# Sums on VectorE issued later in mixer A's values, and the first token tile scaled by its gain behind the transposes

## The chip, the cores and the metric

The kernel runs on one core of one Trainium2 chip. A core has five engines that run their own instruction streams side by side: TensorE (PE, matmuls and transposes), VectorE (DVE), ScalarE (ACT), GpSimd (POOL) and SyncE (SP, which here only issues DMAs). The metric is device time in microseconds (us), as the median of several executions. Besides, one execution was profiled.

## The reference

A two-layer encoder on x of 512 tokens by 1024 channels, float32. Each layer is a token mixer and a squared-ReLU MLP, each behind an RMS norm. Layer 0 has mixer A, attention in three groups of eight heads of 128 columns with different dilations; layer 1 has mixer B, latent attention. Cut to what matters here:

```python
h = rms_norm(x, norm_mix[0])              # x * rsqrt(mean(x*x) + 1e-6) * gain
qkv = (h @ w_qkv).reshape(B, S, 3, N_GROUPS, A_HEADS, A_HEAD_DIM)
for g, (window, dil) in enumerate(DIL_CONFIGS):
    q = rope(rms_norm(qkv[:, :, 0, g], q_gain[g]), S)
    k = rope(rms_norm(qkv[:, :, 1, g], k_gain[g]), S)
    v = qkv[:, :, 2, g]
    o, lse = dilated_group(q, k, v, window, dil)
...
x = x + (o @ w_o);  x = x + sq_relu_mlp(rms_norm(x, norm_ffn[0]), w1, w2)
```

The change touches the norm of x and the product that gives v.

## The kernel before, in words

**Tiling.** The 512 tokens lie in four tiles of 128 rows (r = 0 to 3). A tile is normed by `norm(r)`: ScalarE squares and sums a row (L138), VectorE adds epsilon (L130, `rs_v`), GpSimd raises to the power -0.5 (L133, `nrs`), and one VectorE instruction multiplies x by this scale and by the gain table, a row of 1024 gains copied to all partitions by a DMA (L376, `xn`). `turn(r)` transposes the tile on TensorE in two halves of four 128x128 blocks (L125, into a bank `tp`), so that the channels lie on the partitions.

**Splitting.** Every product is made of three matmuls on rounded operands: hi·hi, hi·lo and lo·hi. ScalarE makes the rounded hi by a copy, and VectorE subtracts it from the value to give lo. For the tokens this is L388 and L389 (`hT`); for weights it is `split_w` (L421 and L422, `whi` and `wlo`, in four buffers each), or L158 and L159 for head 6. For the first two tiles ScalarE also keeps the unrounded turned tile (L392, `h32`).

**The values.** `v_phase` makes v of heads 0 to 5 with a product of 2 by 2 blocks in seven products instead of eight (Strassen's scheme in Winograd's form). The blocks of the weights of a group g are b11, b21, b12 and b22, each 512 rows by 384 columns, loaded in two pieces (L343, 384 KB each). Some products use sums of blocks: bT = b11+b12, then bT+b22, then bT+b21, and b3 = b12+b22. `add_block` (L346) makes such a sum in two VectorE instructions. On the token side sums `Ssp` are made once. The products run in the order 2, 1, 5, 3, 6, 7, 4; each has two halves u of the weights and two blocks t of the tokens. They accumulate in three pairs of banks: `acc` (product 2), `sc` (products 1, 6, 7 and 4) and `tp` (products 5 and 3). `put` (L447) drains a bank into `vo`, by a copy on ScalarE (L453) or an addition or subtraction on VectorE (L455), and a DMA of GpSimd's queue stores the result. After product 6 the `sc` banks are subtracted from `vo`, and product 7 goes on adding to the same banks, so it has to wait for the drain; the same holds between products 7 and 4. `piece(g, ba)` holds products 5 to 4 of a group. Head 6 of all groups is made by a plain product (`block_groups`, L191) between products 1 and 5 of group 0; its weights (`raw`) come in four pairs of DMAs, and the last pair comes last.

**What sets the order.** A scheduler places the instructions of each engine from the program and a model of their times; `tc.issue_after(x)` adds the rule that what stands in it is issued after x. On its engine an instruction then runs strictly in the place given. SP issues its DMAs in order, and each waits until the one eight places before has landed. In the program, the sums of a group stand behind products 2 and 1 of that group, but the scheduler places an instruction as soon as its inputs are expected, so they could move ahead into the group before. After product 1 of group 1, `tables(0)` makes four products for attention A's rotary tables (L271 and L274).

## Time and profile before

| | |
|---|---|
| median of three runs | 1404.27 us (1403.55 to 1405.62) |
| the profiled execution's own time | 1403.76 us |
| its span in the trace | 1402.0 us |
| TensorE busy | 1371.6 us, 98% |
| VectorE busy | 940.0 us, 67% |
| values (`v_phase`) | from the start to about 120 us |
| attention A's first part | 124 to 540 us |

In rows of the waits the columns are: who waited (engine, operation, line), for whom, the sum in us, how often, and the longest. In rows of windows: the window, its length, then for each engine its busy time and instructions, the granted TensorE clock, the busy share of the DMA engines, and GB/s. In rows of a timeline: start, length, engine, line, operation, output and inputs, shapes, count, and in brackets how long the engine was idle before and what ended it.

### The profile page before, as it was taken

How to read it: one execution, taken by the hardware profiler on the slowest of the kernel's cores; microseconds unless marked ns; L12 is line 12 of the kernel's file. 1: busy time of each engine (PE TensorE's matmuls, PEld its weight loads, DVE VectorE, ACT ScalarE, POOL GpSimd, SP SyncE). 2: the span in 40 equal slices, each digit the busy share in tenths (PEclk: the TensorE clock that was granted, in tenths of full speed). 3: DMA queues.
4: the chain of work that ended last, by engine and by line, in shares of the span. 5: the costliest groups of instructions: out<-in, count | busy, mean ns of one | idle time of the engine just before them, and what ended most of it. 6: DMA issues, size and time to landing. Idle time of an engine off the chain costs nothing.

```text
span 1402.0 us, 18979 instructions
## 1 busy us (share of the span) xinstructions
PE 1371.6 (98%) x6852; PEld 1163.6 (83%) x6852; DVE 940.0 (67%) x1498; ACT 801.0 (57%) x1643; POOL 224.0 (16%) x240
## 2 busy tenths in 40 slices
PE   7999999999999999999999999999999999999998
PEld 6999887888889989888888878777769888888887
DVE  6886777787788744464655768788745465574747
ACT  6544778687786624453536455777534553644543
POOL 1110212121122001020200204433201020020101
PEclk9999999999999999999999999999999999999999
DMA  9535553655555539486583944211116668493835
GB/s 309 170 134 163 134 130 97 164 131 125 143 130 120 158 106 271 135 186 174 123 237 87 234 96 95 61 31 31 46 46 189 172 131 230 98 234 119 198 88 120
DMA packets 171774, 197.83 MB, mean 141 GB/s; under 512 B 59104, under 2 KB 109024, under 8 KB 171680
## 3 DMA queue, kind: packets, MB, share of 16 engines
q1 hardware_dynamic: 152496, 157.55, 37.7%
q0 software_dynamic: 19184, 39.07, 15.5%
q8 instruction: 54, 0.88, 0.3%
q14 instruction: 40, 0.33, 0.1%
HBM read 176.13 MB, written 7.86 MB: 131 GB/s over the span
## 4 chain that ended last, share of the span: by engine, by line
PE 80%; DVE 7%; DMA 4%; issue 4%; ACT 3%; POOL 1%; SPq 0%; ACTq 0%; DVEq 0%; POOLq 0%
PE acc L191 49%; PE sc L877 9%; PE tp L877 6%; PE sc L436 3%; PE tp L125 2%; DMA wqs<-in_ffn_w_dram 2%; PE acc L1170 1%; DVE wlo L820 1%; PE sc L1064 1%; DMA xT<-t 1%; PE acc L1146 1%; PE tp L436 1%; PE sc L602 1%; PE sco L716 1%; PE sco L712 1%
## 5 line engine op out<-in xcount | busy, mean ns | idle before, releaser
L191 PE MATMUL acc<-whi,hT 128*128 128x512 f32 (+2 forms) x1208 | 377.2, 388 | 1.9 <-ACT hT L761 1.0
L191 PE MATMUL acc<-hT_f,whi 128*128 128x512 f32 (+1 forms) x1152 | 317.5, 366 | 0.0
L159 DVE TENSOR_TENSOR wlo<-raw,whi 128x1024 fp32r<-128x1024 f32 (+3 forms) x146 | 172.8, 1188 | 169.3 <-ACT whi L158 168.8
L191 PEld LDWEIGHTS acc<-whi,hT 128*128 128x128 f32 x1208 | 224.4, 188 | 42.7 <-ACT hT L761 1.7
L158 ACT ACTIVATE whi<-raw 128x1024 fp32r<-128x1024 f32 (+3 forms) x146 | 149.7, 1029 | 159.6 <-PE acc L191 74.8
L191 PEld LDWEIGHTS acc<-hT_f,whi 128*128 128x128 f32 x1152 | 207.9, 189 | 34.9
L191 PE MATMUL acc<-wlo,hT 128*128 128x512 f32 (+2 forms) x604 | 232.9, 386 | 0.4 <-DVE wlo L159 0.4
L820 DVE TENSOR_TENSOR wlo<-wqs,whi 128x1024 fp32r<-128x1024 f32 x112 | 137.7, 1231 | 114.0 <-ACT whi L819 113.9
L819 ACT ACTIVATE whi<-wqs 128x1024 fp32r<-128x1024 f32 x112 | 118.3, 1060 | 162.0 <-PE acc L191 66.2
L191 PE MATMUL acc<-hT_f,wlo 128*128 128x512 f32 (+1 forms) x576 | 204.1, 366 | 0.0
L877 PE MATMUL sc<-whi,asp 128*128 128x512 f32 x512 | 165.1, 390 | 1.0 <-DVE resid L851 1.0
L805 POOL DMA_DIRECT2D wqs<-in_ffn_w_dram x64 | 77.7, 1347 | 539.7 <-DVE wlo L820 358.1
L191 PEld LDWEIGHTS acc<-wlo,hT 128*128 128x128 f32 x604 | 113.7, 188 | 20.1 <-DVE wlo L159 1.0
L191 PEld LDWEIGHTS acc<-hT_f,wlo 128*128 128x128 f32 x576 | 108.3, 189 | 17.3
L877 PEld LDWEIGHTS sc<-whi,asp 128*128 128x128 f32 x512 | 96.2, 188 | 21.6 <-issue 1.8
L877 PE MATMUL tp<-whi,asp 128*128 128x512 f32 x352 | 112.1, 390 | 0.9 <-DVE resid L851 0.9
L133 POOL TENSOR_TENSOR qrs<-rs_v,nhalf 128x4 f32<-128x4 f32 x48 | 64.6, 1348 | 265.0 <-DVE rs_v L130 241.8
L877 PE MATMUL sc<-wlo,asp 128*128 128x512 f32 x256 | 99.7, 390 | 0.0
L307 ACT ACTIVATE qkT<-xT 128x1024 uint16<-128x1024 uint16 x48 | 56.5, 1181 | 39.5 <-DMA xT<-t 39.4
L877 PEld LDWEIGHTS tp<-whi,asp 128*128 128x128 f32 x352 | 66.1, 188 | 15.0 <-DVE resid L851 1.3
L877 PE MATMUL tp<-wlo,asp 128*128 128x512 f32 x176 | 68.2, 390 | 0.0
L138 ACT ACTIVATE junk<-acc 128x128 f32<-128x128 f32 x192 | 52.3, 273 | 12.3 <-PE acc L191 8.7
(236 smaller groups left out, 2186.8 us busy)
## 6 DMA issues: line engine op xcount, KB each, us to landing
wqs<-in_ffn_w_dram SPq DMA_DIRECT2D x80, 512.0 KB, 5.0
raw<-in_ffn_w_dram SPq DMA_DIRECT2D x64, 512.0 KB, 4.6
wqs<-in_ffn_w_dram POOLq DMA_DIRECT2D x64, 512.0 KB, 7.2
raw<-in_a_w_qkv_dram SPq DMA_DIRECT2D x96, 256.0 KB, 3.2
b<-in_a_w_qkv_dram SPq DMA_DIRECT2D x24, 384.0 KB, 5.7
vall<-vo POOLq DMA_DIRECT2D x24, 192.0 KB, 2.3
raw<-in_a_w_o_dram SPq DMA_DIRECT2D x8, 512.0 KB, 4.1
raw<-in_b_w_o_dram SPq DMA_DIRECT2D x8, 512.0 KB, 3.8
```

Source lines behind the costliest of these rows:

```text
L125: return PE.transpose(o, i, ident)
L133: G.tensor_tensor(out, v[:, :n], nhalf[:, :n], op=ALU.pow)
L138: A.activation(junk, x, AF.Square, scale=1.0 / math.sqrt(dim), accum_out=out)
L158: A.activation(hi[:, :nk, :n], raw[:, :nk, :n], AF.Copy)
L159: V.tensor_tensor(lo[:, :nk, :n], raw[:, :nk, :n], hi[:, :nk, :n].bitcast(F32), op=ALU.subtract)
L191: last = PE.matmul(accs[o][:, oc], lhsT=lt, rhs=rt, start=(kt == 0 and p_i == 0 and hv == 0), stop=(kt == total - 1 and p_i == 2), skip_gr ...
L307: A.activation(dst, xT.rearrange("p (h c) t -> p c t h", h=2), AF.Copy)
L436: PE.matmul(banks[t][:, :VH], lhsT=lt, rhs=rt[:, j], start=(first and k == 0 and i_ == 0), stop=(k == 3 and i_ == 2), skip_group_check=True)
L805: marks["sum"] = nc.gpsimd.dma_start(t, src, accum_op=ALU.add).ins
L819: A.activation(hi, x, AF.Copy)
L820: V.tensor_tensor(lo, x, hi.bitcast(F32), op=ALU.subtract)
L877: PE.matmul(bk[t], lhsT=lt, rhs=rt[:, j], start=(first and k == 0 and i_ == 0), stop=(k == 3 and i_ == 2), skip_group_check=True)
```

## The change

Six edits:

1. `add_block` returns its last instruction, so that others can be placed behind it.
2. At the start, VectorE fills a tile with ones, and TensorE makes twelve 128x128 matmuls on it into a spare bank.
3. The DMAs of the start change places. The gain table came right behind tile 0; now it comes behind tile 1. In its old place stands, behind the identity `ck`, a small DMA of the gains as 8 rows of 128 (`g8`). It is one DMA more, so every later DMA waits on another one eight places before it.
4. Tile 0 is multiplied by its scale alone, in two halves, the second first. TensorE turns `g8` into a column for each 128 channels (`gT`), and behind the transposes VectorE multiplies by it, into `h32`, from which hi and lo are made. ScalarE's copies L392 of tile 0 go.
5. bT of group 0 is made behind the norm of tile 3. In groups 1 and 2, bT's first sum is placed behind the group before's last subtraction and behind the last split of product 2, and b3 behind bT+b22.
6. `tables(0)` is placed behind the last group's sums.

```diff
@@ add_block
-                V.tensor_tensor(t[:, us], x[:, us], y[:, us], op=ALU.add)
+                last = V.tensor_tensor(t[:, us], x[:, us], y[:, us], op=ALU.add)
+            return last.ins
...
+        ones = vp.tile([P, P], F32, name="ones")
+        V.memset(ones, 1.0)
+        spare = acc_p.tile([P, 512], F32, tag="acc", name=nm("spare"))
+        for _ in range(12):
+            PE.matmul(spare[:, 0:P], lhsT=ones, rhs=ones, start=True, stop=True)
         load_x(0)
-        gain_b = gain_table(norm_mix[0:1, :].rearrange("o d -> (o d)"), D, "g_mix0")
         nc.sync.dma_start(ck[:, 0:P], consts[:, 0:P])
+        g8 = vp.tile([KD, P], F32, name="g8")
+        nc.sync.dma_start(g8, norm_mix[0:1, :].rearrange("o (k p) -> (o k) p", p=P))
+        gT = vp.tile([P, KD], F32, name="gT")
         b21[0] = block(0, 1, 0, "b21")
         load_x(1)
+        gain_b = gain_table(norm_mix[0:1, :].rearrange("o d -> (o d)"), D, "g_mix0")
         b11[0] = block(0, 0, 0, "b11")
@@ norm
-            V.scalar_tensor_tensor(xns[r], xts[:, r], rs, gain_b, op0=ALU.mult, op1=ALU.mult)
+            if r:
+                marks["xn"] = V.scalar_tensor_tensor(xns[r], xts[:, r], rs, gain_b, op0=ALU.mult, op1=ALU.mult).ins
+                return
+            for hf in (1, 0):
+                sl = slice(512 * hf, 512 * hf + 512)
+                last = V.tensor_scalar(xns[r][:, sl], xts[:, r, sl], rs, None, op0=ALU.mult)
+            PE.transpose(spare[:, P:P + KD], g8, ident[:KD, :KD])
+            with tc.issue_after(last.ins):
+                marks["gT"] = V.tensor_copy(gT, spare[:, P:P + KD]).ins
@@ turn
-                A.activation(hi, tv, AF.Copy)
-                V.tensor_tensor(lo, tv, hi.bitcast(F32), op=ALU.subtract)
-
+                if r == 0:
+                    with tc.issue_after(marks["gT" if half else "lo"]):
+                        V.tensor_tensor(h32[:, r, sl], tv, gT[:, sl].unsqueeze(2).broadcast_to([P, 4, P]), op=ALU.mult)
+                    tv = h32[:, r, sl]
+                marks["hi"] = A.activation(hi, tv, AF.Copy).ins
+                marks["lo"] = V.tensor_tensor(lo, tv, hi.bitcast(F32), op=ALU.subtract).ins
+
+                if r == 0:
+                    continue
@@ piece
-            add_block(bT[g], bT[g], b22[g])
+            after_t = add_block(bT[g], bT[g], b22[g])
...
-            add_block(b3, b12[g], b22[g])
+            with ExitStack() as behind:
+                if g:
+                    behind.enter_context(tc.issue_after(after_t))
+                add_block(b3, b12[g], b22[g])
...
+            marks["minus", g] = marks["put"]
@@ the main line
         norm(0)
-        split(2, b21[0], 0)
+        with tc.issue_after(marks["gT"]):
+            split(2, b21[0], 0)
         turn(0)
-        split(2, b21[0], 1)
-        norm(1)
+        with tc.issue_after(marks["gT"]):
+            split(2, b21[0], 1)
+        with tc.issue_after(marks["hi"]), tc.issue_after(marks["lo"]):
+            norm(1)
...
-                add_block(bT[0], b11[0], b12[0])
+                with tc.issue_after(marks["xn"]):
+                    add_block(bT[0], b11[0], b12[0])
...
-            add_block(bT[g], b11[g], b12[g])
+            with tc.issue_after(marks["minus", g - 1]), tc.issue_after(seconds):
+                add_block(bT[g], b11[g], b12[g])
             piece(g, ba)
+        with tc.issue_after(marks["sums", NG - 1]):
+            tables(0, g0, rot[:, 0:256], rot[:, 256:768])
```

In the changed kernel the line numbers are higher: L389 is L410, L421 and L422 are L444 and L445, L436 is L459, L455 is L478.

Three places show how the order moves. The first is VectorE at the start; `b_4` is b21 of group 0, `tp` the turned tile. Before, from the first scale on:

```order
L130 TENSOR_SCALAR rs_v_158<-nss_156 128x1
L376 SCALAR_TENSOR_TENSOR xn_110<-xts,nrs_160,g_mix_3_119 128x1024
L422 TENSOR_TENSOR wlo_164<-b_4_122,whi_163 128x2x384
L422 TENSOR_TENSOR wlo_184<-b_4_122,whi_183 128x2x384
L389 TENSOR_TENSOR hT_91<-tp_167,hT_91 128x4x128
L389 TENSOR_TENSOR hT_91<-tp_175,hT_91 128x4x128
L130 TENSOR_SCALAR rs_v_190<-nss_187 128x1
```

The same stretch now:

```order
L130 TENSOR_SCALAR rs_v_176<-nss_174 128x1
L390 TENSOR_SCALAR xn_110<-xts,nrs_178 128x512 x2
L393 COPY gT<-spare_119 128x8
L445 TENSOR_TENSOR wlo_185<-b_4_138,whi_184 128x2x384
L407 TENSOR_TENSOR h_111<-tp_188,gT 128x512
L445 TENSOR_TENSOR wlo_205<-b_4_138,whi_204 128x2x384
L410 TENSOR_TENSOR hT_91<-h_111,hT_91 128x4x128
L407 TENSOR_TENSOR h_111<-tp_196,gT 128x512
L410 TENSOR_TENSOR hT_91<-h_111,hT_91 128x4x128
L130 TENSOR_SCALAR rs_v_211<-nss_208 128x1
```

Two products with the column (`h`) and a copy have come in ahead of tile 1's scale, and the splits of b21 stand between them.

The second place is VectorE at products 6, 7 and 4 of group 0: `b_70` is b3 of group 0, `bT_384` its bT, `b_84`, `b_85` and `b_86` are blocks of group 1 and `bT_671` and `b_110` its sums, `sc_154` and `sc_155` the banks. Before:

```order
L422 TENSOR_TENSOR wlo_584<-b_70_542,whi_583 128x2x384
L455 TENSOR_TENSOR vo<-vo,sc_154 128x384
L349 TENSOR_TENSOR bT_671<-b_84_662,b_85_665 128x768 x2
L422 TENSOR_TENSOR wlo_600<-b_70_542,whi_599 128x2x384
L422 TENSOR_TENSOR wlo_620<-bT_384,whi_619 128x2x384
L455 TENSOR_TENSOR vo<-vo,sc_155 128x384
L422 TENSOR_TENSOR wlo_636<-bT_384,whi_635 128x2x384
L349 TENSOR_TENSOR b_110_824<-b_85_665,b_86_668 128x768 x2
L455 TENSOR_TENSOR vo<-vo,sc_154 128x384
```

Now, with `b_71` as b3, `bT_405` as bT and `sc_172` and `sc_173` as banks:

```order
L445 TENSOR_TENSOR wlo_605<-b_71_563,whi_604 128x2x384
L349 TENSOR_TENSOR bT_405<-bT_405,b_4_138 128x768 x2
L445 TENSOR_TENSOR wlo_621<-b_71_563,whi_620 128x2x384
L445 TENSOR_TENSOR wlo_641<-bT_405,whi_640 128x2x384
L478 TENSOR_TENSOR vo<-vo,sc_172 128x384
L478 TENSOR_TENSOR vo<-vo,sc_173 128x384
L445 TENSOR_TENSOR wlo_657<-bT_405,whi_656 128x2x384
L478 TENSOR_TENSOR vo<-vo,sc_172 128x384
```

The two sums of group 1 are gone from here, and the first subtraction of the bank `sc` has moved behind the splits of product 7's second half and product 4's first. On TensorE, half of product 3, which stood between products 6 and 7, now stands ahead of product 6.

The third place is SP behind the loads of group 0, where `raw` is the last piece of head 6's weights, and the blocks `b` are b21 and b11 of group 1. Before:

```order
L343 DMA b_83_659<-in_a_w_qkv_dram 128x2x384 x2
L146 DMA raw_149<-in_a_w_qkv_dram 128x3x128 x2
L531 DMA rot<-in_consts_dram 128x768
L320 DMA rot<-in_a_q_gain_dram 128x128
L320 DMA rot<-in_a_k_gain_dram 128x128
L343 DMA b_84_662<-in_a_w_qkv_dram 128x2x384 x2
```

Now:

```order
L343 DMA b_84_680<-in_a_w_qkv_dram 128x2x384 x2
L343 DMA b_85_683<-in_a_w_qkv_dram 128x2x384 x2
L146 DMA raw_167<-in_a_w_qkv_dram 128x3x128 x2
L562 DMA rot<-in_consts_dram 128x768
L320 DMA rot<-in_a_q_gain_dram 128x128
L320 DMA rot<-in_a_k_gain_dram 128x128
```

The two pieces of b11 have moved ahead of head 6's last two and of three small loads.

More of the change, by code (lines that the diff above doesn't have):

```diff
@@ L421, in split_w @@
             A.activation(hi, x, AF.Copy)
-            V.tensor_tensor(lo, x, hi.bitcast(F32), op=ALU.subtract)
+            marks["split"] = V.tensor_tensor(lo, x, hi.bitcast(F32), op=ALU.subtract).ins
             return hi, lo
@@ L470, in piece @@
             b3 = vp.tile([P, 4, VH], F32, tag="h32", name=nm("b3"))
-            add_block(b3, b12[g], b22[g])
+            with ExitStack() as behind:
+                if g:
+                    behind.enter_context(tc.issue_after(after_t))
+                add_block(b3, b12[g], b22[g])
             both(6, bT[g], ba, False)
             put(g, 0, 1, "sub", ba, True)
-            add_block(bT[g], bT[g], b21[g])
+            marks["sums", g] = add_block(bT[g], bT[g], b21[g])
             both(7, b3, ba, False)
             put(g, 1, 1, "sub", ba, True)
+            marks["minus", g] = marks["put"]
             both(4, bT[g], ba, False)
@@ L542, in v_phase @@
             both(2, b21[g], bd, True)
+            seconds = marks["split"]
             put(g, 0, 0, "set", bd, False)
@@ L545, in v_phase @@
             put(g, 0, 0, "add", ba, True)
-            if g == 1:
-                with tc.issue_after(marks["put"]):
-                    tables(0, g0, rot[:, 0:256], rot[:, 256:768])
-            add_block(bT[g], b11[g], b12[g])
+            with tc.issue_after(marks["minus", g - 1]), tc.issue_after(seconds):
+                add_block(bT[g], b11[g], b12[g])
             piece(g, ba)
+        with tc.issue_after(marks["sums", NG - 1]):
+            tables(0, g0, rot[:, 0:256], rot[:, 256:768])
     ap0 = tc.tile_pool(name="ap0", bufs=1, reuse_waits="tile")
```

## The prediction

> **What bounds the kernel now.** I read the page's first part, then TensorE's waits up to 130 us (the change touches nothing later except by order), then a table of windows, then the rows of single engines at each wait.
>
> ```profile
> PE 1371.6 (98%) x6852; PEld 1163.6 (83%) x6852; DVE 940.0 (67%) x1498; ACT 801.0 (57%) x1643; POOL 224.0 (16%) x240
> ...
> PE tp L125 <- DVE xn L376: 8.9, 1, 8.9
> PE sc L436 <- DVE vo L455: 1.0, 3, 0.6
> PE sc L436 <- DVE wlo L422: 0.6, 1, 0.6
> PE acc L436 <- DVE hT L389: 0.2, 1, 0.2
> PE acc L436 <- ACT hT L388: 0.2, 1, 0.2
> ...
> 19.18:41.19 22.01, 22.01 (x132) 21.91 (x133) 20.45 (x31) 15.51 (x27) 1.87 (x3) 1.00 0.83 274
> 41.19:59.74 18.55, 17.72 (x99) 16.70 (x98) 18.55 (x25) 9.84 (x16) 3.31 (x5) 1.00 0.50 154
> 85.63:124.24 38.61, 38.61 (x221) 38.39 (x222) 26.91 (x34) 19.05 (x27) 7.01 (x13) 1.00 0.23 79
> 124.24:540.00 415.76, 411.37 (x2210) 354.14 (x2210) 305.94 (x591) 287.72 (x786) 67.59 (x54) 1.00 0.53 139
> ```
>
> TensorE is busy for 98% of the span, so only its idle time and its slow time can be won. After the 8.9 us of the start it waits 2.0 us up to 130 us. VectorE works all 18.55 us of the second window: there, and only there, it sets the pace. So removed VectorE work is worth at most the waits that it causes.
>
> **The start.** Rows of the first two tiles, from GpSimd, VectorE and TensorE (start, length, and in brackets the idle time before and who ended it):
>
> ```profile
> 6.21 0.56 POOL L133 TENSOR_TENSOR nrs<-rs_v,nhalf 128x1 f32<-128x1 f32 x1 [5.77 <-DVE rs_v L130]
> ...
> 7.58 1.28 DVE L376 SCALAR_TENSOR_TENSOR xn<-xts,nrs,g_mix 128x1024 f32<-128x1024 f32 x1 [1.45 <-DMA g_mix<-in_norm_mix_dram]
> 12.68 0.14 DVE L130 TENSOR_SCALAR rs_v<-nss 128x1 f32<-128x1 f32 x1
> 13.49 1.28 DVE L376 SCALAR_TENSOR_TENSOR xn<-xts,nrs,g_mix 128x1024 f32<-128x1024 f32 x1 [0.67 <-POOL nrs L133]
> 14.70 1.82 DVE L422 TENSOR_TENSOR wlo<-b,whi 128x768 fp32r<-128x768 f32 x2
> 18.44 1.28 DVE L389 TENSOR_TENSOR hT<-tp,hT 128x512 fp32r<-128x512 f32 x2
> ...
> 8.91 1.97 PE L125 MATMUL tp<-ck,xn 128*128 128x128 f32 x8 [8.91 <-DVE xn L376]
> 15.27 1.03 PE L125 MATMUL tp<-ck,xn 128*128 128x128 f32 x8
> 16.06 0.42 PE L436 MATMUL sc<-wlo,hT 128*128 128x384 f32 x1
> 19.18 0.62 PE L436 MATMUL acc<-whi,hT 128*128 128x384 f32 x2 [0.24 <-DVE hT L389]
> ```
>
> The power of the first tile is ready at 6.21+0.56=6.77, but the product with the gain waits for the table until 7.58. In the changed kernel that wait of 0.8 us is gone, and the transposes of the second half need only half a scaling. But that gain must survive tile 1. The new chain holds more VectorE work: two products with the column (a 128x512 operation, 0.64 each, half of the 1.28 row) and a small copy, and ScalarE's hi's now wait for them. ScalarE loses two copies, but its square of tile 1 stands behind the hi's of tile 0. Working the instructions off in the new order, with the durations above, I get the scale of tile 1 at 13.06 instead of 12.68. Its norm starts 0.81 later (13.49-12.68), at 13.87, and ends at 15.15; TensorE's transposes start at 15.2 and take 0.8 (16.06-15.27). Then the 2.9 us of products that stood between 16.06 and 18.94 follow, so TensorE reaches the point of 19.18 at about 18.9. The lo's of tile 1 no longer stand behind the norm of tile 2: 13.87 + 1.20 (norm) + 1.74 (two splits) + 0.75 give the first at 17.6, in time. The start is worth **-0.3**, between -1.0 (the 0.8 survives whole, and some slow time goes) and +0.5 (tile 1's norm 0.4 later, felt in full).
>
> Those numbers take TensorE at its fast pace from 15.2. The trace has a slow time, though not in the granted clock, which the table gives as 1.00:
>
> ```profile
> 11.00:14.30 3.30, 3.08 (x8) 1.00 1.06 388
> 14.30:18.90 4.60, 4.60 (x29) 1.00 1.19 306
> ```
>
> Eight matmuls in 3.08 us against 29 in 4.60 (some of them short): the change to the fast pace came some 5.4 us after the first transpose at 8.91. Twelve matmuls on ones are put ahead of it. At the slow 1.97/8=0.25 us they take 3.0 us; then TensorE is idle for about 3 us until the transposes. If they raise the pace, some products of tile 0 run earlier, but tile 1's norm bounds the gain as above. If they don't, the change comes 5.4 us after the new first transpose at 7.3, at 12.7, still ahead of 15.2.
> [...]
>
> **Sums moved back.** Rows of the second window, where VectorE is full, and the waits that end there:
>
> ```profile
> 52.14 0.85 ACT L421 ACTIVATE whi<-b 128x768 fp32r<-128x768 f32 x1 [1.53 <-PE sc L436]
> ...
> 52.49 0.54 DVE L455 TENSOR_TENSOR vo<-vo,sc 128x384 f32<-128x384 f32 x1
> 52.95 1.81 DVE L349 TENSOR_TENSOR bT<-b,b 128x768 f32<-128x768 f32 x2
> 54.69 0.95 DVE L422 TENSOR_TENSOR wlo<-b,whi 128x768 fp32r<-128x768 f32 x1
> 55.56 0.95 DVE L422 TENSOR_TENSOR wlo<-bT,whi 128x768 fp32r<-128x768 f32 x1
> 57.76 1.81 DVE L349 TENSOR_TENSOR b<-b,b 128x768 f32<-128x768 f32 x2
> ...
> 51.94 0.51 PE L436 MATMUL tp<-whi,Ssp 128*128 128x384 f32 x2
> 53.67 0.33 PE L436 MATMUL sc<-whi,Ssp 128*128 128x384 f32 x1
> 55.69 0.45 PE L436 MATMUL sc<-wlo,Ssp 128*128 128x384 f32 x1 [0.64 <-DVE wlo L422]
> 57.02 0.44 PE L436 MATMUL sc<-whi,Ssp 128*128 128x384 f32 x1 [0.19 <-DVE vo L455]
> 60.09 0.44 PE L436 MATMUL sc<-whi,hT 128*128 128x384 f32 x1 [0.21 <-DVE vo L455]
> 85.63 0.41 PE L436 MATMUL sc<-whi,Ssp 128*128 128x384 f32 x1 [0.62 <-DVE vo L455]
> ```
>
> The sums of group 1 (52.95 and 57.76, 1.81 each) stand in the middle of group 0's last products: the split at 54.69 had its hi at 52.14+0.85=52.99 and still waited, and TensorE with it (0.64). These 3.6 us leave, and all four waits can go: 0.64+0.19+0.21+0.62 = **-1.66**. In their new place the sums lie beside products 2 and 1 of their own group, where the row of 85.63 shows VectorE at 26.91 of 38.61 us and TensorE without idle time; the same holds for the four table products, 0.68 each. So they cost nothing there; without that cover each pair of sums would cost its 1.81.
>
> What is late next is a drain. Before, ten matmuls of product 3 stood between product 6's last and product 7's first (51.94 to 53.67, 1.73 us), while VectorE drained the bank. In the new order product 7 follows product 6 at once, and the first subtraction stands behind two splits, that of product 7's second half and of product 4's first. The latter's hi needs the buffer of product 6's first half, free 12 matmuls (2.08 us at 0.173) ahead of the end. From there hi 0.85, lo 0.87, subtraction 0.54 and some 0.2 of hand-over are 2.46: TensorE waits **0.4** in each of three groups, **+1.2** in all. Bounds: 0 for each, if the scheduler's places hold with buffers free earlier, and 1.5 (52.99 + 0.87 + 0.87 + 0.46 = 55.2 against 53.67) where VectorE comes late. I take 0.4, which the chain gives when VectorE is free.
>
> **A queue that was reordered.** SP takes the second block of group 1 ahead of the last two pieces of head 6 (raw at 23.49).
>
> ```profile
> 23.49 0.90 SPq L146 DMA_DIRECT2D raw<-in_a_w_qkv_dram  x2
> 25.98 1.82 SPq L343 DMA_DIRECT2D b<-in_a_w_qkv_dram  x2
> ...
> 29.11 0.85 ACT L158 ACTIVATE whi<-raw 128x768 fp32r<-128x768 f32 x1 [0.87 <-DMA raw<-in_a_w_qkv_dram]
> 29.99 0.96 DVE L159 TENSOR_TENSOR wlo<-raw,whi 128x768 fp32r<-128x768 f32 x1 [0.43 <-ACT whi L158]
> ...
> 33.36 0.34 PE L191 MATMUL acc<-wlo,hT 128*128 128x384 f32 x1
> ...
> 20.00:28.00 8.00, 8.00 (x51) 7.97 (x51) 7.55 (x10) 4.76 (x9) 1.74 (x3) 1.00 1.09 352
> ```
>
> The pieces landed just ahead of 29.11. The DMA engines are full there (352 GB/s), and 786 KB more ahead of them are 2.2 us: they land at 31.3, hi and lo end at 33.1. TensorE wants the lo at 33.4, less 0.3 for the start, so it just holds or waits a little. But VectorE idles meanwhile, and gives back 1.3 to 2.2 of the 3.6 us that it gained. I take **+0.2**, from 0 (they land as before) to +1.5 (product 5's first split, due at 41.19, comes that much late).
>
> **The sum.** -0.3 -1.7 +1.2 +0.2 = -0.6, on the profiled execution's 1403.76 (span 1402.0, 1.8 outside it): 1403.2. The median of three is 1404.27, 0.5 above, so for a median 1403.7. The scheduler also reshuffles instructions in attention A; that stage has 415.76-411.37=4.4 us of idle time in all, after which the order is the same. I give it 0 with ±1.5.
>
> **Rivals.**
> - TensorE alone sets the pace. If head 6's pieces land in time and the drain costs nothing, the waits all go: -1.66 -1.0 = -2.7, 1401.6, and with a good reshuffle about 1400.8. For it speaks that VectorE has 3.6 us less; against it the two splits ahead of the subtraction.
> - The drain is late in every group. If VectorE enters product 6 late because of head 6's pieces, it has the two splits still to do when product 6 ends, and each group waits up to 1.5 instead of 0.4: 4.5 -1.7 -0.3 +0.5 = +3.0, 1407.3, slower. It decides from the point where VectorE is over 0.4 us behind at the end of product 6. For it: VectorE had not one idle moment from 41.19 to 59.74. Against it: groups 1 and 2 have the cover of 85.63.
> - The warm-up fails and the pace falls back besides. The 15 matmuls or so behind 15.2 would run at about 0.32 instead of 0.17, +2.3, and the eight transposes +1.0, less the 1.66 of waits that a later TensorE no longer has: +1.6, 1405.9. [...] No row of before shows an idle time behind a fast stretch that long, so this has 0.07.
> - The change does nothing: the drains take over the waits whole, and the start loses at tile 1 what it won: 1404.3.
>
> **How the numbers follow.** A difference under 0.2% (2.8 us) can hardly be told from no change. Forecast (1402.4 to 1405.2) 0.53; TensorE's pace 0.20; the late drain 0.12; the pace that falls back 0.07; nothing 0.08. Predicted 1403.7. The range reaches from the first rival with a good reshuffle to just short of the second: 1400.8 to 1406.9. Faster, below 1401.5: four in ten of the first rival and 0.12 of the forecast's tail with reshuffles over -1.5, 0.2. Slower, above 1407.1: most of the late drain and a little of the third, 0.13. The rest, 0.67, is the same.
>
> **What would show it.** The norm of tile 0 right behind the power, at 6.8; tile 1's scale at 13.1; TensorE at the point of 19.18 by 18.9. Head 6's last hi on ScalarE at about 31.3. In each group one wait of TensorE on the subtraction of 0.4 at the start of product 7, and none on a split. I am wrong if TensorE stands idle over 1 us anywhere between 30 and 60 us, if the subtraction costs over 1 us in groups 1 or 2, or if attention A changes by more than 1.5 us.

## The result and the profile after

| | before | changed |
|---|---|---|
| median of six runs each, same chip | 1404.55 us (1403.55 to 1405.62) | 1414.68 us (1413.38 to 1416.65) |
| ratio, with its 95% interval | | 1.0074 [1.0061, 1.0087] |
| the profiled execution's own time | 1403.76 us | 1413.38 us |
| its span | 1402.0 us | 1411.6 us |

The change makes the kernel 10 us slower. The forecast was 1403.7, with a range that ended at 1406.9. First, TensorE on the page of the changed kernel, and then its waits up to 130 us (who waited, for whom, sum, how often, longest):

```profile
PE 1379.5 (98%) x6877; PEld 1168.2 (83%) x6877; DVE 942.4 (67%) x1503; ACT 801.0 (57%) x1641; POOL 229.5 (16%) x240
```

```profile
PE acc L459 <- ACT hT L409: 2.1, 1, 2.1
PE sc L459 <- DVE vo L478: 1.8, 3, 0.8
...
PE acc L191 <- DVE wlo L159: 0.4, 1, 0.4
PE tp L459 <- DVE wlo L445: 0.3, 1, 0.3
```

Before, TensorE waited 1.0 on the subtraction and 0.6 on a split in group 0; now it waits 1.8 on three subtractions and 0.3 on a split. Nothing here is worth 9 us. Two landmarks tell where the time went: the last drain of the values on VectorE, and the first norm of the MLP behind attention A (group rows by line; what counts are the first and last start). Before:

```profile
L455 DVE TENSOR_TENSOR vo<-vo,sc x18: 539/546/555, 25.1 to 119.2; 128x384 f32<-128x384 f32 x18
...
L227 DVE SCALAR_TENSOR_TENSOR xn<-resid,nrs,g_ffn x8: 1274/1284/1285, 518.9 to 1072.5; 128x1024 f32<-128x1024 f32 x8
```

Changed:

```profile
L478 DVE TENSOR_TENSOR vo<-vo,sc x18: 547/548/555, 24.5 to 120.6; 128x384 f32<-128x384 f32 x18
...
L227 DVE SCALAR_TENSOR_TENSOR xn<-resid,nrs,g_ffn x8: 1277/1283/1287, 528.1 to 1081.8; 128x1024 f32<-128x1024 f32 x8
```

The values end 1.4 us later (120.6-119.2), attention A 9.2 later (528.1-518.9), and the last MLP norm, 554 us on, 9.3 later. So the stage between, **attention A, lost 7.8 us**, though no line of the change is in it; behind it nothing was lost.

To place the loss within the stage, where the two orders differ, I gave every matmul its median duration in the trace of before and compared the times at which both traces had done equal work. The changed kernel is behind by 1.4 us at 124, about 6 at 200, 2.5 at 280, 3.3 at 460, 4.4 at 490 and 9.3 at 500, and stays there. Most of the loss near 200 is made up; that between 460 and 500, 6.0 us, stays. Windows of both (length, then busy time of PE, PEld, DVE, ACT, POOL, granted clock, DMA share, GB/s); before, then changed:

```profile
120.00:212.00 92.00, 91.85 (x438) 77.19 (x437) 63.53 (x116) 62.53 (x171) 17.37 (x15) 1.00 0.58 156
...
440.00:507.00 67.00, 65.50 (x418) 60.30 (x417) 45.22 (x85) 39.18 (x105) 2.39 (x2) 1.00 0.59 167
```

```profile
120.00:212.00 92.00, 88.73 (x417) 72.94 (x416) 61.47 (x111) 59.96 (x164) 16.62 (x14) 1.00 0.56 151
...
440.00:516.00 76.00, 71.09 (x428) 64.08 (x427) 49.62 (x95) 42.69 (x122) 4.04 (x4) 0.98 0.49 147
```

TensorE's idle time went from 0.15 to 3.27 us in the first and from 1.50 to 4.91 in the last; and there the granted clock fell to 0.98.

What happens there is the end of a chain: q and k of the last heads are projected, rotated, transposed by DMAs, copied by ScalarE (L307, `qkT`), turned into scores, and the shares of the groups merged (`mx`, `scm`, `me`); with them P is scaled, transposed and multiplied by v. Rows of the last part of it, before (VectorE, then TensorE):

```profile
471.82 0.17 DVE L663 TENSOR_TENSOR mx<-stat 128x8 f32<-128x8 f32 x1
...
482.61 0.15 DVE L683 COPY me<-scm 128x8 f32<-128x8 f32 x1
485.01 2.34 DVE L688 TENSOR_TENSOR P<-P,me 128x1024 f32<-128x1024 f32 x2
...
490.30 1.04 PE L125 MATMUL tp<-ck,P 128*128 128x128 f32 x8
```

Changed:

```profile
485.17 0.16 DVE L694 TENSOR_TENSOR mx<-stat 128x8 f32<-128x8 f32 x1
...
494.82 0.16 DVE L714 COPY me<-scm 128x8 f32<-128x8 f32 x1
496.62 2.35 DVE L719 TENSOR_TENSOR P<-P,me 128x1024 f32<-128x1024 f32 x2
...
491.88 0.84 PE L191 MATMUL acc<-whi,hT 128*128 128x512 f32 x3
492.56 0.39 PE L191 MATMUL acc<-wlo,hT 128*128 128x512 f32 x1
...
493.47 0.39 PE L191 MATMUL acc<-whi,hT 128*128 128x512 f32 x1
493.70 0.50 PE L713 MATMUL scm<-ca,xsel 128*128 128x4 f32 x4
494.06 1.07 PE L125 MATMUL tp<-ck,P 128*128 128x128 f32 x8
495.63 0.49 PE L743 MATMUL sco<-pT,vt 128*128 128x128 f32 x2 [0.50 <-DVE pT L729]
497.99 0.63 PE L125 MATMUL tp<-ck,P 128*128 128x128 f32 x4 [1.87 <-DVE P L719]
499.30 1.12 PE L125 MATMUL tp<-ck,P 128*128 128x128 f32 x4 [0.69 <-ACT pT L736]
```

Before, the first of the last two scalings of P was done at 485.01+1.17=486.2, and its eight transposes ran at 490.30: 4.1 us of slack, which projections (L191) and products with v filled. Now the chain is 13.4 late at `mx` (485.17-471.82), and the scaling begins 11.6 later, at 496.62; its eight transposes, the rows of 497.99 and 499.30, start 7.7 later than before, about 11.6 less the slack. The projections have run out (the last at 493.47) when `scm` comes, and TensorE waits 0.50, 1.87 and 0.69. Then the clock falls; windows of TensorE alone, changed kernel (length, busy time, granted clock, DMA share, GB/s):

```profile
495.34:498.75 3.41, 1.11 (x6) 1.00 0.69 170
498.75:502.16 3.41, 2.86 (x14) 0.50 0.92 326
```

2.3 us of idle time in the first 3.41 us (3.41-1.11) are followed by 3.41 us at a granted clock of 0.50, which by my estimate cost some 1.4 more (half of the 2.86 us of work in them).

### The profile page after: what moved, and what is told of

Its sections match the earlier page's. It is cut to its first block, busy times and chain, and to the rows that moved or that the text cites. A ratio compares the mean times of both kernels' runs of the same rounds, so it can differ in the third digit from the quotient of the medians.

```text
span 1411.6 us, 19043 instructions
## 1 busy us (share of the span) xinstructions
PE 1379.5 (98%) x6877; PEld 1168.2 (83%) x6877; DVE 942.4 (67%) x1503; ACT 801.0 (57%) x1641; POOL 229.5 (16%) x240
## 4 chain that ended last, share of the span: by engine, by line
PE 75%; DVE 10%; ACT 7%; DMA 4%; issue 4%; POOL 0%; SPq 0%; DVEq 0%; ACTq 0%; POOLq 0%
PE acc L191 41%; PE sc L908 11%; PE tp L908 7%; DMA xT<-t 3%; PE sc L459 3%; PE tp L125 2%; PE acc L1201 1%; PE sc L1095 1%; PE acc L1177 1%; ACT t L299 1%; ACT P L644 1%; ACT junk L138 1%; DVE wlo L851 1%; ACT whi L158 1%; DVE wlo L445 1%
## 5 line engine op out<-in xcount | busy, mean ns | idle before, releaser
L191 PE MATMUL acc<-whi,hT 128*128 128x512 f32 (+2 forms) x1208 | 376.8, 388 | 3.2 <-ACT hT L792 1.0
L191 PE MATMUL acc<-hT_f,whi 128*128 128x512 f32 (+1 forms) x1152 | 317.2, 366 | 0.0
L191 PEld LDWEIGHTS acc<-whi,hT 128*128 128x128 f32 x1208 | 224.6, 188 | 45.7 <-ACT hT L1203 1.5
L191 PEld LDWEIGHTS acc<-hT_f,whi 128*128 128x128 f32 x1152 | 207.8, 189 | 35.0
L191 PE MATMUL acc<-wlo,hT 128*128 128x512 f32 (+2 forms) x604 | 232.4, 386 | 0.4 <-DVE wlo L159 0.4
L191 PE MATMUL acc<-hT_f,wlo 128*128 128x512 f32 (+1 forms) x576 | 203.9, 365 | 0.0
L191 PEld LDWEIGHTS acc<-wlo,hT 128*128 128x128 f32 x604 | 113.6, 188 | 19.9 <-DVE wlo L159 0.9
L191 PEld LDWEIGHTS acc<-hT_f,wlo 128*128 128x128 f32 x576 | 108.2, 189 | 17.3
L133 POOL TENSOR_TENSOR qrs<-rs_v,nhalf 128x4 f32<-128x4 f32 x48 | 71.0, 1483 | 262.9 <-DVE rs_v L130 230.6
L307 ACT ACTIVATE qkT<-xT 128x1024 uint16<-128x1024 uint16 x48 | 56.6, 1181 | 40.3 <-DMA xT<-t 40.1
L299 ACT ACTIVATE t<-t 128x1024 uint16<-128x1024 uint16 x48 | 50.0, 1051 | 18.4 <-DVE t L297 18.4
```

Of the source, the lines that this page charges most:

```text
L133: G.tensor_tensor(out, v[:, :n], nhalf[:, :n], op=ALU.pow)
L191: last = PE.matmul(accs[o][:, oc], lhsT=lt, rhs=rt, start=(kt == 0 and p_i == 0 and hv == 0), stop=(kt == total - 1 and p_i == 2), skip_gr ...
L299: A.activation(halves.rearrange("p (h n) -> p h n", h=2), t1.rearrange("p c d -> p (c d)").bitcast(U16).rearrange("p (n h) -> p h n", h=2) ...
L307: A.activation(dst, xT.rearrange("p (h c) t -> p c t h", h=2), AF.Copy)
```

## Experiments: whose order is it

Every kernel below computes the whole result. All ratios are to runs of the kernel before on the same chip, and two kernels are compared by their ratios. E1 to E12 are numbered in the sequence in which they ran. The rule in question is `issue_after(after_t)`, which puts the sums `b3` behind `bT`+`b22`; the changed kernel has it for groups 1 and 2.

**E1. The changed kernel, with the rule for group 1 alone.**

```diff
-                if g:
+                if g == 1:
                     behind.enter_context(tc.issue_after(after_t))
```

> The changed kernel, with the rule that b3 is placed behind bT+b22 kept for group 1 alone (the changed kernel has it for groups 1 and 2). The scheduler then gives attention A the order of the kernel before on every engine, and TensorE's order in the values stays that of the changed kernel. By work done, the changed kernel is 1.4 us behind at 124 us of the trace of before and 9.3 behind at 540 us. Order theory (attention A's new order costs the 7.8 us between): 1406 to 1407 us, behind by 1.4 at 124 us and by no more than 1.5 to 2 at 540. Value theory (what the values do, their drains, the queue or the low granted clock, is carried on and costs later): 1412 to 1415.

Measured: 1407.63 us against 1406.05, ratio 1.0015 [1.0006, 1.0024]. Without the rule the sums b3 of group 2 come ahead of a drain, as E3 will show, and TensorE waits 1.78 us there, at 88.35.

**E2. The kernel before, with nothing but the rule for group 2.** `add_block` returns its last instruction, as in the change.

```diff
-            add_block(bT[g], bT[g], b22[g])
+            after_t = add_block(bT[g], bT[g], b22[g])
...
-            add_block(b3, b12[g], b22[g])
+            with ExitStack() as behind:
+                if g == 2:
+                    behind.enter_context(tc.issue_after(after_t))
+                add_block(b3, b12[g], b22[g])
```

> The kernel before, with nothing added but the rule that b3 of group 2 is placed behind bT+b22. Nine matmuls of product 6 move behind half of product 3 in group 2; attention A gets exactly the order of the changed kernel. Order theory: 1411.5 to 1413, the loss all between 124 and 520 us. Value theory: 1404 to 1405, as before, since start, sums and queue are those of before.

Measured: 1413.16 us, ratio 1.0056 [1.0043, 1.0069]. Its landmarks:

```profile
L456 DVE TENSOR_TENSOR vo<-vo,sc x18: 546/551/556, 25.4 to 120.6; 128x384 f32<-128x384 f32 x18
...
L227 DVE SCALAR_TENSOR_TENSOR xn<-resid,nrs,g_ffn x8: 1277/1284/1286, 526.7 to 1080.6; 128x1024 f32<-128x1024 f32 x8
```

It is 1.4 late at the end of the values and 7.8 at the end of attention A: the stage loses 6.4 us. One placing rule, on two sums that VectorE has time for, makes most of the loss, and without it (E1) the stage loses 0.4 (121.9-119.2=2.7 late at its start, 522.0-518.9=3.1 at its end). The orders say how. In attention A, E1 has the order of the kernel before, and E2 that of the changed kernel. From E1 to the changed kernel little moves up to the end of the values: on TensorE nine matmuls of product 6 of group 2 come behind product 3, on VectorE the two sums and a few rows around them. In attention A hundreds of TensorE's instructions stand elsewhere, and behind it none. VectorE, at three places in the order of the program (- E1, + changed; the last is the first difference in attention A, where `rs_v` belongs to the norm of q and k):

```
-L349 TENSOR_TENSOR b_151_1115<-b_126_960,b_127_963 128x768 x2
 L445 TENSOR_TENSOR wlo_919<-bT_692,whi_918 128x2x384
...
 L349 TENSOR_TENSOR bT_966<-bT_966,b_127_963 128x768
+L349 TENSOR_TENSOR b_151_1115<-b_126_960,b_127_963 128x768 x2
...
+L130 TENSOR_SCALAR rs_v_1390<-qss_1379 128x4
 L297 TENSOR_TENSOR t_183_1352<-t_183_1352,qrs_1359 128x512
-L130 TENSOR_SCALAR rs_v_1390<-qss_1379 128x4
```

The scheduler places the next instruction by its model of times. I read the difference so: a small shift at the end of the values decides another choice at the start of attention A, and each choice shifts the next. In the order that results, the last q and k projection has its four accumulators end nearly together (matmuls 2066 to 2103 from the kernel's start, without the twelve on ones and the transpose of `g8`, which only the changed kernel has) where they ended one after another (2003 to 2088), and the last `scm` is matmul 2295 instead of 2255. At 0.68/3=0.23 us each (the rows at 491.88 and 492.56) 40 matmuls are 9.2 us. With the 3.3 us that TensorE was behind at 460 anyway that makes 12.5, and the copy behind `scm` came 12.2 later (494.82-482.61). The groups of L307 show the same chain; before, E1, E2 and changed:

```profile
L307 ACT ACTIVATE qkT<-xT x48: 1161/1182/1195, 148.5 to 463.3; 128x1024 uint16<-128x1024 uint16 x48
```

```profile
L307 ACT ACTIVATE qkT<-xT x48: 1164/1184/1199, 152.2 to 466.5; 128x1024 uint16<-128x1024 uint16 x48
```

```profile
L307 ACT ACTIVATE qkT<-xT x48: 1155/1181/1194, 152.6 to 474.3; 128x1024 uint16<-128x1024 uint16 x48
```

```profile
L307 ACT ACTIVATE qkT<-xT x48: 1162/1182/1194, 153.3 to 476.0; 128x1024 uint16<-128x1024 uint16 x48
```

The last copy comes 11.0 and 12.7 late under the new order, 3.2 under the old one.

**E9. The changed kernel, with the values of the last head held back as filler.** `v_last`, a projection without a chain behind it, is put behind a rotary product of the last q and k.

```diff
-        V.tensor_tensor(t15, a5, cosg[g][:, r].unsqueeze(2).broadcast_to([P, 2, 2, DH]), op=ALU.mult)
+        marks["qk"] = V.tensor_tensor(t15, a5, cosg[g][:, r].unsqueeze(2).broadcast_to([P, 2, 2, DH]), op=ALU.mult).ins
...
-        v_last(*vs)
+        with tc.issue_after(marks["qk"]):
+            v_last(*vs)
```

> The changed kernel, where head 7's product at the end of attention A is placed behind the last evacuation of the last q and k projection. In the changed kernel its matmuls stand among those of that projection, whose four tiles so end together and late, and the scores, the softmax and the last scaling of P come about 10 us later than in the kernel before, when no block product is left to fill TensorE (4 us idle and 3.4 us of low clock from 494 to 502 us). Late-chain theory: the last scores stand 20 matmuls earlier (about 4 us), the scaling with them, and of the 4.8 us lost between 490 and 500 us at least 2 come back: 1411 to 1413 where the changed kernel has 1414.7, ratio 1.004 to 1.006. Rival (the loss there is only the fallen clock, or hangs on something else): ratio as the changed kernel's, 1.0074.

Measured: 1416.50 us against 1405.17, ratio 1.0082 [1.0068, 1.0096]; nothing came back. At equal work it is 2.5 behind at 430, 9.1 at 460, 10.1 at 500. TensorE near 460:

```profile
459.97 0.71 PE L633 MATMUL sc<-qkT 128*128 128x128 f32 x4 [2.92 <-ACT qkT L307]
...
462.06 1.22 PE L633 MATMUL sc<-qkT 128*128 128x128 f32 x4 [1.20 <-ACT qkT L307]
```

The filler now covers the end of the chain, and is missing where it covered an earlier wait, on `qkT`. The loss moved 40 us ahead and kept its size, and the clock fell there instead (0.50 from 461.49 to 464.90). The edit brings the last `scm` only 11 of the 40 matmuls forward. So it is not the place of this one projection: the chain is late, and which single choice makes it late stays open.

## Experiments: the values and the start

In this table each kernel's landmarks stand against those of before (119.2 and 518.9), from group rows like the ones above; they are of one execution each. How far single executions differ shows in the kernel before, E3 and E5, whose orders are alike up to 50 us: TensorE's 101st matmul starts at 28.50, 30.04 and 29.26. So a difference of 1.5 us between two landmarks decides nothing alone. Besides, the execution of before in the profile (1403.76) is the second fastest of its six.

| kernel | ratio [95%] | end of values | end of attention A |
|---|---|---|---|
| changed | 1.0074 [1.0061, 1.0087] | +1.4 | +9.2 |
| E1: rule for group 1 alone | 1.0015 [1.0006, 1.0024] | +2.7 | +3.1 |
| E3: sums and tables alone | 0.9994 [0.9986, 1.0003] | +0.7 | +1.4 |
| E5: E3, b3 of group 2 later still | **0.9983 [0.9973, 0.9992]** | -1.5 | -0.1 |
| E4: first tile's edits alone | 1.0025 [1.0014, 1.0037] | +4.7 | +6.7 |
| E6: E4 without the ones | 1.0023 [1.0014, 1.0032] | +2.7 | +2.4 |
| E7: changed, b3 as in E5 | 1.0009 [1.0000, 1.0018] | +0.7 | +1.4 |
| E8: E7, head 6's loads first | 1.0006 [0.9997, 1.0015] | +1.5 | +3.0 |
| E10: E7, more ones | 1.0028 [1.0017, 1.0040] | +1.7 | +2.9 |
| E11: E7, gain table loaded as before | 0.9995 [0.9986, 1.0004] | -0.8 | +0.4 |
| E12: E7 without the ones | 1.0007 [0.9998, 1.0016] | +1.6 | +1.7 |

**E3. The kernel before, with the sums and the tables moved alone** (edits 1, 5 and 6, the rule for group 1 only, so that attention A keeps its order).

```diff
+            with ExitStack() as behind:
+                if g == 1:
+                    behind.enter_context(tc.issue_after(after_t))
+                add_block(b3, b12[g], b22[g])
...
+                with tc.issue_after(marks["xn"]):
+                    add_block(bT[0], b11[0], b12[0])
...
+            with tc.issue_after(marks["minus", g - 1]), tc.issue_after(seconds):
+                add_block(bT[g], b11[g], b12[g])
             piece(g, ba)
+        with tc.issue_after(marks["sums", NG - 1]):
+            tables(0, g0, rot[:, 0:256], rot[:, 256:768])
```

> The kernel before with the sums moved (bT of groups 0 to 2, the tables, b3 of group 1), without the edit on the first tile, and with attention A in the order of before. Order theory: 1404 to 1405.5; waits of TensorE on the splits and on the drain at product 7 up to 60 us fall from 1.0 to about 0.5, and a wait of about 0.7 in group 2 comes in. If the sums are what costs (value theory): 1406 or more, behind by over 1.5 at 124 us.

Measured: 1405.07 us against 1406.05. One wait stands out, at product 7 of group 1 (TensorE and VectorE):

```profile
82.98 1.83 DVE L349 TENSOR_TENSOR b<-b,b 128x768 f32<-128x768 f32 x2
...
85.59 1.01 DVE L456 TENSOR_TENSOR vo<-vo,sc 128x384 f32<-128x384 f32 x2
...
86.29 0.41 PE L437 MATMUL sc<-whi,Ssp 128*128 128x384 f32 x1 [1.78 <-DVE vo L456]
```

The sums b3 of group 2, which no rule holds here, have come in between the splits ahead of the drain. So the rule whose side effect cost 6.4 us in attention A was needed where it stood.

**E5. The same, with b3 of group 2 behind the last subtraction of group 1.** This too keeps them out of that place, and leaves attention A's order as it was.

```diff
                 if g == 1:
                     behind.enter_context(tc.issue_after(after_t))
+                elif g == 2:
+                    behind.enter_context(tc.issue_after(marks["minus", 1]))
```

> The sums alone as in the third run, but b3 of group 2 is placed behind group 1's last subtraction. In the third run TensorE waited 1.95 us at product 7 of group 1, and the two instructions of b3 of group 2 stood ahead of the subtraction that it waited for. Attention A keeps the order of before. Drain theory (the sums of the next group ahead of the drain are what costs): this wait falls under 0.6, and the time is 1.3 to 1.6 us under the third run's, a ratio of 0.998 to 0.999 to the kernel before. Rival (the two splits ahead of the drain cost as much by themselves): the wait stays over 1.2, ratio as in the third run, 0.9994.

Measured: 1403.45 us against 1405.30: faster than both kernels. The wait is now

```profile
84.17 0.41 PE L437 MATMUL sc<-whi,Ssp 128*128 128x384 f32 x1 [0.45 <-DVE vo L456]
```

and the values end 1.5 us earlier. Of the 2.2 us between E3 and E5 this wait is 1.3; 0.8 was there at the 101st matmul. The profiled execution gives all but 0.1 of the 1.5 back in attention A. There ScalarE's copies wait for the DMA transposes (39.2 us in 26 waits; before 39.4 in 27); that these hold the stage back whatever its start is not shown. The median kept 1.85 us of gain nevertheless; the profiled execution was the slowest of the eleven, so how much of the gain survives the stage stays open.

**E4 and E6. The first tile's edits alone (2, 3 and 4), and without the ones.** The second diff is against the first.

```diff
+        for _ in range(12):
+            PE.matmul(spare[:, 0:P], lhsT=ones, rhs=ones, start=True, stop=True)
         load_x(0)
-        gain_b = gain_table(norm_mix[0:1, :].rearrange("o d -> (o d)"), D, "g_mix0")
...
+            for hf in (1, 0):
+                sl = slice(512 * hf, 512 * hf + 512)
+                last = V.tensor_scalar(xns[r][:, sl], xts[:, r, sl], rs, None, op0=ALU.mult)
```

```diff
-        for _ in range(12):
-            PE.matmul(spare[:, 0:P], lhsT=ones, rhs=ones, start=True, stop=True)
```

> The kernel before with the edit on the first tile alone (ones, gain column, the changed DMA order), sums, tables and attention A's order as before. In the changed kernel TensorE was 0.7 us behind at 25 us, so if nothing gives it back: 1405.2, behind by 0.7 at 25 us and at 124 us. If the lower granted clock near 11 to 14 us costs more than that later: over 1406. If the first tile's edit gains as meant: 1403.5.

> The first tile's edit alone, without the twelve matmuls on ones. If these raise the pace of TensorE for the first products, taking them out costs: behind at 25 us by over 0.5 more than with them (1.4), ratio over 1.003. If they only move the slow 3.4 us to the first products, nothing changes: behind by 1.0 to 1.8 at 25 us, ratio 1.002 to 1.003; the products between 10 and 14 us run at about 0.32 each either way.

Measured: 1409.53 us (against 1406.05) and 1408.89 (against 1405.30). By themselves the first tile's edits make the kernel slower, and the ones change nothing. The time is lost in one place above all, product 7 of group 0 (TensorE in E6; E4 has the same wait of 2.53 at 58.76):

```profile
58.29 0.41 PE L457 MATMUL sc<-whi,Ssp 128*128 128x384 f32 x1 [2.53 <-DVE vo L476]
```

In E6 product 7 follows product 6 at once, and VectorE makes a sum of group 1, which these two kernels leave in its old place (54.98, 1.82 us), ahead of the subtraction that TensorE waits for. In E4 the clock fell behind this wait besides (0.50 from 58.75 to 62.16), in E6 it did not; at up to half of these 3.41 us, an estimate, that makes most of the 2.0 us between their landmarks.

**E7. The changed kernel with the b3 of E5**, so with attention A's order as before.

```diff
-                if g:
+                if g == 1:
                     behind.enter_context(tc.issue_after(after_t))
+                elif g == 2:
+                    behind.enter_context(tc.issue_after(marks["minus", 1]))
```

> The changed kernel with b3 of group 2 placed behind group 1's last subtraction instead of behind its own bT+b22. Attention A has the order of before; the drain of group 1 is free of sums. Against the first run (1.0015) the wait of 1.95 at 86 us goes: 1.2 to 1.5 us less, ratio 1.0003 to 1.0008; what is left is the start and group 0, behind by 1.5 to 1.8 at 60 us. Rival: as the first run.

Measured: 1406.81 us against 1405.30. Another place for two sums takes back 0.0065 of the changed kernel's 0.0074. Against E5, on the same chip, what is left of the change is the first tile, and it costs 0.0026 here too.

**E8. That, with head 6's last loads ahead of group 1's second block on SP.**

```diff
+        raw3 = marks["raw"]
...
-            b11[g] = block(g, 0, 0, "b11")
+            with tc.issue_after(raw3):
+                b11[g] = block(g, 0, 0, "b11")
```

> The run before, and b11 of group 1 is loaded behind head 6's last two pieces, as in the kernel before. Queue theory (head 6's pieces land 2.2 us late and VectorE idles 1.8 us for them at 32 us, which comes up as TensorE's waits between 41 and 57 us): VectorE's idle time at 30 us falls to 0.5, TensorE is behind by no more than 0.7 at 57 us against 2.5 to 3.5, and ends 0.7 to 1.0 earlier than the run before. Rival (VectorE catches up by itself, because the sums are gone): the same time within 0.4 us.

Measured: 1406.18 us, ratio 1.0006 beside 1.0009, well within the intervals. The place in the queue is worth nothing that can be measured.

**E10. E7, with ten more matmuls on ones behind tile 0's transposes**, to hold the clock up to the first product.

```diff
         turn(0)
+        for _ in range(10):
+            PE.matmul(spare[:, 0:P], lhsT=ones, rhs=ones, start=True, stop=True)
```

> The changed kernel with b3 of group 2 placed late (the seventh run, 1.0009), and ten more matmuls on ones between the first tile's transposes and its first product, so that TensorE has no idle time of 2 us there. In the seventh run the granted clock was at half from 9.6 to 19.9 us. Pace theory (the first tile's edit costs because TensorE falls back to half clock before the products): the clock stays full, the products between 10 and 15 us run at 0.17 instead of 0.32 each, TensorE is behind by 0.6 us or less at 25 us instead of 2.0, ratio 0.9993 to 1.0003. Chain theory (tile 1's norm comes late on VectorE and ScalarE, whatever TensorE's pace): full clock, but TensorE waits for tile 1 longer, behind by 0.8 to 1.5 at 25 us, ratio 1.0004 to 1.0010.

Measured: 1408.60 us against 1405.17. The clock (windows of TensorE) and TensorE at the start of this kernel:

```profile
13.25:16.66 3.41, 1.32 (x9) 1.00 1.10 358
16.66:20.07 3.41, 3.41 (x14) 0.50 1.19 305
```

```profile
14.57 0.44 PE L459 MATMUL sc<-whi,hT 128*128 128x384 f32 x1 [1.03 <-ACT whi L444]
16.07 1.40 PE L125 MATMUL tp<-ck,xn 128*128 128x128 f32 x8 [1.06 <-DVE xn L386]
```

Tile 0's products ran at 0.17 us each, the fast pace, and TensorE then waited 1.03 for a hi and 1.06 for tile 1's norm, and behind these waits the granted clock was 0.50 (16.66 to 20.07). So the pace of tile 0's products is not what limits the start; what a full clock for tile 1 would give, this run does not tell. That this run is slower than E7 by 0.0019 was in neither theory, and I have no explanation that a run tests.

**E11 and E12. E7 with the gain table loaded behind tile 0 again, and E7 without the ones.**

```diff
         load_x(0)
+        gain_b = gain_table(norm_mix[0:1, :].rearrange("o d -> (o d)"), D, "g_mix0")
...
         load_x(1)
-        gain_b = gain_table(norm_mix[0:1, :].rearrange("o d -> (o d)"), D, "g_mix0")
```

```diff
-        for _ in range(12):
-            PE.matmul(spare[:, 0:P], lhsT=ones, rhs=ones, start=True, stop=True)
```

> The seventh run (the changed kernel with b3 of group 2 late, 1.0009), with the gain table loaded in its old place right behind tile 0. The sums alone with b3 late were 0.9983, so the first tile's edit costs 0.0026 (3.6 us) there. Queue theory (that cost comes from the changed order of loads: b12 later, head 6's last pieces behind b11 of group 1): ratio 0.9980 to 0.9992. Chain theory (it comes from the longer way of tile 0 through VectorE and ScalarE, which makes tile 1 late): ratio 1.0005 to 1.0015; tile 0's split of b21 waits about 1.5 us longer for its load, so it may come out slower still.

> The seventh run without the twelve matmuls on ones. The seventh run's granted clock was at half from 9.6 to 19.9 us, behind the ones; the kernels without ones came to full clock between 14.3 and 17.8 us. Pace theory (the ones make the slow time longer, and this is what is left of the cost): ratio 0.9985 to 1.0000, behind by under 1.2 at 25 us. Chain theory (the ones change nothing, as in the runs with the first tile alone, 1.0025 and 1.0023): ratio 1.0003 to 1.0015.

Measured: 1404.68 and 1406.57 us against 1405.36. The order of the loads makes 0.0014 of the 0.0026, about half, which lies between the theories; the ones again nothing. But E11 changes more than the loads: its TensorE order has ten matmuls of product 3 between products 6 and 7 of group 0 again, as the kernel before, and it does not wait there. In E7 product 7 follows product 6 at once:

```profile
56.53 0.41 PE L459 MATMUL sc<-whi,Ssp 128*128 128x384 f32 x1 [0.69 <-DVE vo L478]
```

So part of what the loads cost comes by way of the order. What the rest of the first tile's cost hangs on stays open: no run took the scaling behind the transposes out by itself.

## Why the prediction was wrong

**The step that failed** is the last sentence of the sum: "The scheduler also reshuffles instructions in attention A; that stage has 415.76-411.37=4.4 us of idle time in all, after which the order is the same. I give it 0 with ±1.5." It measured +7.8 us of the 9.2 us that the profiled execution lost up to there. The reshuffle was seen, and the wrong number was taken to bound it: idle time in a stage bounds what a new order can win there, and says nothing of what it can lose. What bounds it is the slack of the stage's chain, and the trace of before had it: 4.1 us between the scaled P and its transposes at 490.30. Counting on TensorE's order how much later `scm` stands (40 matmuls, 9.2 us) would have put the loss there at 9.2-4.1=5.1 us; the half clock that followed adds an estimated 1.4. Measured between 460 and 500 it is 6.0, and 6.4 in the whole stage of E2. This sum was made after the result. The other 1.9 us (1.4 behind at 124, 3.3 at 460) it does not explain. E1 and E2 show that the order is the cause, and the rule for group 2 the cause of the order.

**The start** was forecast as -0.3 and is a loss. Rows of the changed kernel (VectorE, ScalarE, TensorE):

```profile
6.73 0.88 DVE L390 TENSOR_SCALAR xn<-xts,nrs 128x512 f32<-128x512 f32 x2 [0.68 <-POOL nrs L133]
...
12.56 0.69 DVE L410 TENSOR_TENSOR hT<-h,hT 128x512 fp32r<-128x512 f32 x1 [0.70 <-ACT hT L409]
13.60 0.15 DVE L130 TENSOR_SCALAR rs_v<-nss 128x1 f32<-128x1 f32 x1 [0.35 <-ACT xn L138]
...
31.49 0.85 ACT L158 ACTIVATE whi<-raw 128x768 fp32r<-128x768 f32 x1 [1.65 <-DMA raw<-in_a_w_qkv_dram]
...
7.36 1.07 PE L125 MATMUL tp<-ck,xn 128*128 128x128 f32 x8 [0.59 <-DVE xn L390]
10.51 0.58 PE L459 MATMUL acc<-whi,hT 128*128 128x384 f32 x1 [2.08 <-ACT hT L409]
...
15.85 1.06 PE L125 MATMUL tp<-ck,xn 128*128 128x128 f32 x8 [1.06 <-DVE xn L386]
...
19.36 0.51 PE L459 MATMUL acc<-whi,hT 128*128 128x384 f32 x2
```

The norm of tile 0 follows the power at 6.73, as forecast (6.8). But tile 1's scale comes at 13.60 instead of 13.06: VectorE waits 0.70 for ScalarE's second hi and 0.35 for its square of tile 1, and the working off had come out 0.54 earlier. From there it runs as forecast, 0.5 late: transposes at 15.85 (15.2), the point of 19.18 at 19.36 (18.9). So TensorE is 0.2 behind there (19.36 against 19.18), 0.5 off the forecast of -0.3. The price of these edits by the medians is 0.0023 to 0.0026 of the time, over 3 us, and part of it comes later, at the drain of group 0: 2.53 in E4 and E6, 0.69 in E7. Half of it goes with the order of the loads (E11), for which the sum had only the 0.2 of the queue.

**The sums and the drains** came out as forecast in kind, and a little worse in size. The new waits are three, one in each group, on the subtraction ahead of product 7: 0.81, 0.45 and 0.55, 1.8 in all against 1.2. The splits' waits are gone but for 0.3, and no wait between 30 and 60 us is over 1 us. So in the changed kernel these waits grew by 0.4 (1.8+0.3-1.66), where the terms -1.7 and +1.2 made -0.5. The late drain of the second rival came in other kernels: where b3 slipped in (E1 and E3, 1.78) and where the sums stayed in their old place (E4 and E6, 2.53). In E5, with b3 late and the first tile as before, the only wait left up to 130 us, behind the start, is the one of 0.45, and the values end 1.5 earlier.

**The queue.** Head 6's last hi came at 31.49, forecast 31.3. VectorE stood idle 1.80 us for it, within the 1.3 to 2.2 of the forecast, and TensorE did not wait for its lo: the wait of 0.4 on a lo of head 6 in the list above is at 24.61, for an earlier piece. The sum had +0.2 for this; E8 finds nothing that can be measured.

**The clock.** The rival in which the pace falls back had 0.07. That an idle time of about 3 us between the ones and tile 0 lowers the pace was an assumption; no row of before shows it, and in the changed kernel TensorE was idle there for only 0.59 (the row at 7.36), at a granted clock of 1.00. Windows of the changed kernel's start show that the clock did fall, but ahead of where the rival put it:

```profile
1.00:7.20 6.20, 5.69 (x25) 1.00 0.78 227
7.23:10.64 3.41, 1.20 (x9) 1.00 0.89 329
10.64:14.05 3.41, 3.41 (x11) 0.50 1.02 373
```

Behind the ones the pace was the faster one: tile 0's eight transposes take 1.07 us (7.36) instead of 1.97. Then comes the wait of 2.08 for tile 0's hi, and its products run at a granted clock of 0.50 up to 14.05. The rival's cost did not come: behind 15.2 the clock was full again (1.00 from 14.05), the eight transposes at 15.85 took 1.06 (before 1.03), and the fifteen products from 16.67 to 19.36 ran at 0.18 each, not at 0.32. Neither leaving out the ones (E6 and E12) nor holding the clock up to the first product (E10) made the kernel faster.

## What to carry to other kernels

A rule that fixes one instruction at the end of a stage can make a scheduler deal the whole next stage anew. So compare the orders stage by stage, and where one differs, look up how far the links of that stage's longest chain have moved and set this against the slack between each link and its use: idle time there bounds the gain alone. Here that sum gives 5.1 us, 6.5 with the clock, against 6.0 measured; it is one case. Count only what moved: instructions that the change adds ahead of the stage shift the numbers without shifting the order. If a rule is needed, try another place that does the same work and keeps the next stage's order; here that took back 0.0065 of the time (E7).

## What the hardware showed

- In the changed kernel TensorE worked 1.20 us of the 3.41 us up to 10.64 and 1.11 of those up to 498.75, in E10 1.32 of those up to 16.66; in the 3.41 us behind each of these the granted clock was 0.50. Near 500 us the loss so came in two parts, as idle time (2.3 us from 495.34) and as clock (an estimated 1.4 behind it).
- How long the clock stayed low differs: 3.41 us in the changed kernel's start (10.64 to 14.05), 10.24 in E7's (9.64 to 19.88).
- The twelve float32 matmuls on ones appear as 24 in the trace, 5.49 us from 1.08 on. With the small transpose of `g8` they fill 5.69 us, where the prediction took 3.0 for the twelve.
